# One helper for u in both layers: the high part written by ScalarE from PSUM, the low part as the difference

## The chip, the core and the metric

The kernel runs on one core of a Trainium2 chip. The engines named below are PE (TensorE, the matmuls; PEld is its weight load), DVE (VectorE), ACT (ScalarE), POOL (GpSimd) and SP (SyncE, whose queue issues nearly all DMAs). The metric is the device time of one execution in microseconds (us); less is better.

## The reference, cut to what matters

A trunk of two layers over a sequence of 256 frames of width 2048, inner width 4096. Layer 0 mixes by chunked gated linear attention, layer 1 by a complex diagonal state space (S5). Both begin alike:

```python
shift, scale, gate = jnp.split(mod[i], 3, axis=-1)
u = x * (1.0 + scale[:, None, :]) + shift[:, None, :]
...
h = gla_mixer(u, ...)    # i = 0: proj = u @ w_in
h = s5_mixer(u, ...)     # i = 1: proj = u @ w_in
x = layer_norm(DEEPNORM_ALPHA * x + (1.0 + gate[:, None, :]) * h, ln_g[i], ln_b[i])
```

Only the way in which u is prepared for the first matmuls of each layer differs between the two kernels.

## The kernel before

Every large matmul is made of three products of a reduced type (fp32r): an operand is split in a high part (a cast) and a low part (the operand minus its high part), and high times high, high times low and low times high are summed. So u is kept as four tiles, transposed, with the channels on the partitions: `u0h`, `u0l` in layer 0 and `u1h`, `u1l` in layer 1, 16 slices k of 128 x 256 each.

The weights stream in blocks of 128 x 1024 (two k, called one step kp): SP issues the load (`wload`, L136), ACT casts the high part (L145) and DVE subtracts for the low part (L146); hi and lo sit in rings of buffers. The steps that use u are `mv_step` (L167 to L169, the projection v: 12 matmuls of 128 x 512 a step) and `st_step` (L180 to L182, q and k, z, and in layer 1 su: 24 matmuls of 128 x 256 a step). L167 and L180 take high by high, L168 and L182 the weight's low part, L169 and L181 u's low part.

Layer 0's u comes in blocks of two, two, four and eight k as the conditioning vector's columns arrive. `u_tr` transposes x on PE into a PSUM bank `psx`, two k side by side in one bank (L363). `u_fin` then, for each k: DVE reads PSUM and writes `uf` = x times scale plus shift (L370), ACT casts `uf` to `u0h` (L351), DVE subtracts (L352). Between blocks, the projections v, q and k are computed over the k at hand, and DVE also sums the adaLN rows (L267).

Layer 1's u comes at one place, about 765 to 784 us: after the layer norm's last pass on DVE (L1007) PE transposes into `psn` (L1028, one k per bank, three banks in turn), ACT reads PSUM and writes `vf` (L1030), casts it to `u1h` (L351), and DVE subtracts for `u1l` (L352). Meanwhile PE begins the first group of su, eight steps kp0 to kp7, with the weights of kp0 and kp1 split earlier. Then the temporary pool `tmp0` is closed and `tmp1` takes its place (`tp.close()`, `tp.open("tmp1")`): the tables `rb` of the state space's input matrices (`bload`, L1050 and L1052) lie where `uf` lay, so their loads wait for the last reader of it. From `rb` DVE forms `wb` (`b_pow`, L1090 to L1092), which PE transposes into `pswb` (`b_tr`, L1101).

The order of the instructions on each engine is not that of the source: a scheduler with a cost model of its own sorts them once, and each engine then runs its row in that fixed order, waiting where it must. A change of a few lines can re-sort the row of every engine.

Of the kernel before, what the change touches and what calls it, by code (L numbers as in the profile page):

```python
# [8 lines left out]
F32 = mybir.dt.float32  # L9
F32R = mybir.dt.float32r  # L10
AF = mybir.ActivationFunctionType
ALU = mybir.AluOpType
# [3 lines left out]
P = 128  # L16
D = 2048
E = 4096
T = 256
# [14 lines left out]
def trunk(ctx, tc, x, c, ln_g, ln_b, ada_w, ada_b, gla_w_in, gla_gate_w2, gla_gate_b, gla_norm_g,  # L34
# [3 lines left out]
    V, S, PE = nc.vector, nc.scalar, nc.tensor  # L38
# [32 lines left out]
    tp = Phase()  # L71
    tp.open("tmp0")

    def s8t(name, shape, dt=F32):
        return s8.tile([P] + shape, dt, tag="s8", name=name)
# [4 lines left out]
    def psx(name):  # L80
        return ax.tile([P, 512], F32, tag="ax", name=name)
# [141 lines left out]
    ps = psx("psc")  # L223
# [6 lines left out]
    mods = cp.tile([P, 2, 2, 16], F32, name="mods")  # L230
# [117 lines left out]
    u0 = Parts([s8t(f"u0h{i}", [8, T], F32R) for i in range(2)], [s8t(f"u0l{i}", [8, T], F32R) for i in range(2)])  # L348

    def hilo(hi, lo, src):  # L350
        S.copy(hi, src)  # L351
        V.tensor_tensor(lo, src, hi.bitcast(F32), op=ALU.subtract)  # L352

    vbig = bigp.tile([P, 8448], F32, tag="big", name="vbig")
    vtok = vbig[:, :8192].rearrange("p (j e) -> p j e", j=2)
    win = gla_w_in[0]
# [9 lines left out]
    def u_fin(k2, ps):  # L366
        for kk in range(2):
            k = k2 + kk
            uf = tp.tile([P, T], F32, tag="uf", name=f"uf{k}", bufs=2)
            V.tensor_scalar(uf, ps[:, kk * T:(kk + 1) * T], mods[:, 0, 1, k:k + 1], mods[:, 0, 0, k:k + 1], op0=ALU.mult, op1=ALU.add)  # L370
            hilo(u0.hi(k), u0.lo(k), uf)

    qk = [s8t(f"qk{i}", [8, T]) for i in range(2)]

# [72 lines left out]
    ps = psx("psv2")  # L447
# [8 lines left out]
    got = []  # L456
    ada_now(0, 1, *blocks[0], rows=[8, 4, 4], between=lambda: got.append(u_tr(0)))()
    u_fin(0, got[0])


# [315 lines left out]
    def put_u(k2, at):  # L776
        got = []
        put(at, lambda: got.append(u_tr(k2)))
        put(at, lambda: u_fin(k2, got[0]))
# [50 lines left out]
    for c0, w_, o in ((0, 4, 0), (1, 3, 4), (2, 2, 7)):  # L830
        a = s8t(f"qs{c0}", [8, w_, 64])
# [10 lines left out]
    for h in range(4):  # L842
        ps = psx(f"psst{h}")
# [173 lines left out]
    ab1 = cp.tile([P, 2, 16], F32, name="ab1")  # L1017
# [6 lines left out]
    u1 = Parts([s8t(f"u1h{i}", [8, T], F32R) for i in range(2)], [s8t(f"u1l{i}", [8, T], F32R) for i in range(2)])  # L1024
    for k in range(16):
        ps = psx(f"psn{k}")
        for tt in range(2):
            PE.transpose(ps[:, tt * P:(tt + 1) * P], res0[tt][:, k * P:(k + 1) * P], ident)  # L1028
        uf = tp.tile([P, T], F32, tag="uf", name=f"vf{k}", bufs=2)
        S.activation(uf, ps[:, :T], AF.Identity, scale=ab1[:, 0, k:k + 1], bias=ab1[:, 1, k:k + 1])  # L1030
        hilo(u1.hi(k), u1.lo(k), uf)

    tp.close()
    rp.close()
# [391 lines left out]
    ps = psx("psnb")  # L1426
# [33 lines left out]
```

## Time and profile before

| | |
|---|---|
| time, median of 3 (lowest, highest) | 1846.15 us (1845.58, 1850.67) |
| profiled execution: its own time, span of the trace | 1846.54 us, 1844.7 us |
| busy share of the span, PE / DVE / ACT | 97% / 77% / 49% |
| chain that ended last, share of the span, PE / DVE / DMA / ACT | 86% / 8% / 3% / 2% |

The profiled execution is 0.39 us above the median and within the spread of the three. The span is the traced part of the execution, 1.8 us shorter than its time. PE is busy nearly throughout, so what counts is where it is not: the places in which PE waits for another engine, and the stretches with a lower granted clock.

### The profile page before, as it was taken

Reading aid. Unit: us, or ns where it says so; the run is one execution under the profiler, and the core shown is the slowest. Engines: PE = TensorE matmul, PEld = TensorE weight load, DVE = VectorE, ACT = ScalarE, POOL = GpSimd, SP = SyncE. Lnnn points to the kernel's source line nnn. Section 1 sums busy time; section 2 is a strip of 40 time slices with the busy share of each in tenths; the row PEclk is TensorE's granted clock in tenths of the full one; section 3 lists DMA queues with packets and bytes.
Section 4 is the critical chain, followed back from the end, with each engine's and each line's share of the span. In section 5 each row is a group of like instructions: output and inputs, shape, how many; then the busy total and the mean of one; then the engine's idle time right before and its main releaser. Section 6 shows DMA issues by size and latency. Waiting matters only on the chain.

```text
span 1844.7 us, 33886 instructions
## 1 busy us (share of the span) xinstructions
PE 1795.5 (97%) x13619; PEld 1588.5 (86%) x13619; DVE 1422.5 (77%) x1890; ACT 897.4 (49%) x1252; POOL 72.7 (4%) x78
## 2 busy tenths in 40 slices
PE   7999999999999999999999999999999999999997
PEld 5776897899999888899999999988888888888885
DVE  4877657879989888697899689888677775557556
ACT  5433557556556333654454454545544444444332
POOL 0000000000000000002223200000000000000000
PEclk9999999999999999999999999999999999999999
DMA  9996875889889998465654477899688886668653
GB/s 343 386 333 248 294 244 164 279 261 325 291 286 317 333 353 281 163 220 158 183 151 147 139 214 222 235 246 238 224 276 264 276 271 206 191 189 325 194 184 92
DMA packets 243798, 449.48 MB, mean 244 GB/s; under 512 B 19572, under 2 KB 48942, under 8 KB 242358
## 3 DMA queue, kind: packets, MB, share of 16 engines
q1 hardware_dynamic: 239320, 436.02, 73.9%
q0 software_dynamic: 3552, 10.24, 1.8%
q8 instruction: 107, 1.75, 0.4%
q10 hardware_dynamic: 768, 1.05, 0.2%
q14 instruction: 51, 0.42, 0.1%
HBM read 432.81 MB, written 14.42 MB: 242 GB/s over the span
## 4 chain that ended last, share of the span: by engine, by line
PE 86%; DVE 8%; DMA 3%; ACT 2%; issue 2%; SPq 0%; DVEq 0%; ACTq 0%
PE gl L192 13%; PE gl L193 7%; PE op L168 6%; PE op L167 6%; PE op L169 6%; PE z L182 3%; PE z L180 3%; PE z L181 3%; PE sz L180 3%; PE v L168 3%; PE v L169 3%; PE sz L181 3%; PE sz L182 3%; PE v L167 3%; PE su L180 2%; PE su L182 2%
## 5 line engine op out<-in xcount | busy, mean ns | idle before, releaser
L146 DVE TENSOR_TENSOR logl<-wgl,higl 128x1024 fp32r<-128x1024 f32 x128 | 156.5, 1224 | 115.3 <-ACT higl L145 113.7
L145 ACT CAST higl<-wgl 128x1024 fp32r<-128x1024 f32 x128 | 134.4, 1051 | 172.2 <-PE gl L192 167.9
L192 PE MATMUL gl<-yb,higl 128*128 128x512 f32 x512 | 179.6, 395 | 0.0
L192 PE MATMUL gl<-yp,higl 128*128 128x512 f32 x512 | 179.3, 395 | 0.1
L145 ACT CAST hio<-wo 128x1024 fp32r<-128x1024 f32 x95 | 100.2, 1055 | 155.3 <-PE op L169 127.3
L146 DVE TENSOR_TENSOR loo<-wo,hio 128x1024 fp32r<-128x1024 f32 x95 | 116.2, 1225 | 67.2 <-ACT hio L145 63.7
L315 DVE SCALAR_TENSOR_TENSOR acc<-wa,cs,acc 128x512 f32<-128x512 f32 x217 | 162.2, 748 | 4.8 <-DMA wa<-in_ada_w 2.1
L180 PE MATMUL su<-u1h,hisu 128*128 128x256 f32 x512 | 153.5, 301 | 1.9 <-DVE vv L1108 1.9
L180 PE MATMUL sz<-u1h,hisz 128*128 128x256 f32 x512 | 149.7, 292 | 1.2 <-ACT zs L1290 1.2
L180 PE MATMUL z<-u0h,hiz 128*128 128x256 f32 x512 | 148.7, 290 | 0.0
L182 PE MATMUL su<-u1h,losu 128*128 128x256 f32 x512 | 145.7, 286 | 0.4 <-DVE losu L146 0.4
L181 PE MATMUL su<-u1l,hisu 128*128 128x256 f32 x512 | 145.8, 285 | 0.0
L182 PE MATMUL z<-u0h,loz 128*128 128x256 f32 x512 | 144.9, 283 | 0.6 <-DVE loz L146 0.6
L182 PE MATMUL sz<-u1h,losz 128*128 128x256 f32 x512 | 144.9, 283 | 0.0
L181 PE MATMUL sz<-u1l,hisz 128*128 128x256 f32 x512 | 144.7, 283 | 0.0
L181 PE MATMUL z<-u0l,hiz 128*128 128x256 f32 x512 | 144.7, 283 | 0.0
L193 PE MATMUL gl<-yb,logl 128*128 128x256 f32 x512 | 143.4, 280 | 0.0
L193 PE MATMUL gl<-yp,logl 128*128 128x256 f32 x512 | 142.0, 280 | 0.0
L145 ACT CAST hisz<-wsz 128x1024 fp32r<-128x1024 f32 x64 | 66.9, 1051 | 107.2 <-PE sz L181 55.1
L192 PEld LDWEIGHTS gl<-yb,higl 128*128 128x128 f32 x512 | 96.0, 188 | 22.6
L192 PEld LDWEIGHTS gl<-yp,higl 128*128 128x128 f32 x512 | 95.8, 188 | 22.6 <-issue 0.6
L145 ACT CAST hisu<-wsu 128x1024 fp32r<-128x1024 f32 x64 | 66.7, 1050 | 95.1 <-PE su L181 70.6
(322 smaller groups left out, 5019.8 us busy)
## 6 DMA issues: line engine op xcount, KB each, us to landing
wgl<-in_s_w_glu SPq DMA_DIRECT2D x128, 512.0 KB, 4.7
wa<-in_ada_w SPq DMA_DIRECT2D x116, 512.0 KB, 5.1
wv<-in_gla_w_in SPq DMA_DIRECT2D x64, 512.0 KB, 6.1
wz<-in_gla_w_in SPq DMA_DIRECT2D x64, 512.0 KB, 5.2
wsu<-in_s_w_in SPq DMA_DIRECT2D x64, 512.0 KB, 3.7
wsz<-in_s_w_in SPq DMA_DIRECT2D x64, 512.0 KB, 4.3
wo<-in_s_w_out SPq DMA_DIRECT2D x64, 512.0 KB, 4.5
a<-in_ada_w SPq DMA_DIRECT2D x31, 1024.0 KB, 10.7
```

The costliest lines, as they stand in the source:

```text
L145: S.copy(hi, w)
L146: last_lo[0] = V.tensor_tensor(lo, w, hi.bitcast(F32), op=ALU.subtract).ins
L167: PE.matmul(banks[tt], lhsT=uh, rhs=hi[:, kk, :], start=(k == first), stop=False)
L168: PE.matmul(banks[tt], lhsT=uh, rhs=lo[:, kk, :], start=False, stop=False)
L169: last_mm[0] = PE.matmul(banks[tt], lhsT=ul, rhs=hi[:, kk, :], start=False, stop=(k == last)).ins
L180: PE.matmul(o, lhsT=wh, rhs=u.hi(k), start=(k == first), stop=False)
L181: PE.matmul(o, lhsT=wh, rhs=u.lo(k), start=False, stop=False)
L182: last_mm[0] = PE.matmul(o, lhsT=wl, rhs=u.hi(k), start=False, stop=(k == last)).ins
L192: PE.matmul(banks[f], lhsT=hi[:, kk, fs], rhs=u.both(k), start=(k == 0), stop=False)
L193: PE.matmul(banks[f][:, :T], lhsT=lo[:, kk, fs], rhs=u.hi(k), start=False, stop=(k == last))
L315: V.scalar_tensor_tensor(acc[0], w[:, kk, :], cs[:, k:k + 1], acc[0], op0=ALU.mult, op1=ALU.add)
```

## The change

A new helper `affine_hilo` is used in both layers. ACT computes the affine function straight from PSUM into the high part (L357, an ACTIVATE with scale and bias and a reduced output), DVE computes the same function from the same PSUM slice into `uf` (L358, scale and add in one TENSOR_SCALAR), and DVE subtracts (L359). In layer 0 this replaces DVE's multiply-add, ACT's cast of it, and DVE's subtraction: the same three kinds of work, with the cast's source changed. In layer 1 it replaces ACT's activation, ACT's cast and DVE's subtraction: ACT issues one instruction fewer per k, DVE one more. The two reads of a PSUM slice are put one behind the other, ACT's first (the DVE instruction waits for ACT's). Lines behind L371 are 3 to 5 higher in the kernel after (L1007 becomes L1012, L1050 becomes L1053, L1101 becomes L1104).

```diff
--- before.py
+++ after.py
@@ -351,6 +351,13 @@
         S.copy(hi, src)
         V.tensor_tensor(lo, src, hi.bitcast(F32), op=ALU.subtract)
 
+    def affine_hilo(u, k, src, a, b):
+
+        uf = tp.tile([P, T], F32, tag="uf", name=f"uf{k}", bufs=2)
+        S.activation(u.hi(k), src, AF.Identity, scale=a, bias=b)
+        V.tensor_scalar(uf, src, a, b, op0=ALU.mult, op1=ALU.add)
+        V.tensor_tensor(u.lo(k), uf, u.hi(k).bitcast(F32), op=ALU.subtract)
+
     vbig = bigp.tile([P, 8448], F32, tag="big", name="vbig")
     vtok = vbig[:, :8192].rearrange("p (j e) -> p j e", j=2)
     win = gla_w_in[0]
@@ -366,9 +373,7 @@
     def u_fin(k2, ps):
         for kk in range(2):
             k = k2 + kk
-            uf = tp.tile([P, T], F32, tag="uf", name=f"uf{k}", bufs=2)
-            V.tensor_scalar(uf, ps[:, kk * T:(kk + 1) * T], mods[:, 0, 1, k:k + 1], mods[:, 0, 0, k:k + 1], op0=ALU.mult, op1=ALU.add)
-            hilo(u0.hi(k), u0.lo(k), uf)
+            affine_hilo(u0, k, ps[:, kk * T:(kk + 1) * T], mods[:, 0, 1, k:k + 1], mods[:, 0, 0, k:k + 1])
 
     qk = [s8t(f"qk{i}", [8, T]) for i in range(2)]
 
@@ -1026,9 +1031,7 @@
         ps = psx(f"psn{k}")
         for tt in range(2):
             PE.transpose(ps[:, tt * P:(tt + 1) * P], res0[tt][:, k * P:(k + 1) * P], ident)
-        uf = tp.tile([P, T], F32, tag="uf", name=f"vf{k}", bufs=2)
-        S.activation(uf, ps[:, :T], AF.Identity, scale=ab1[:, 0, k:k + 1], bias=ab1[:, 1, k:k + 1])
-        hilo(u1.hi(k), u1.lo(k), uf)
+        affine_hilo(u1, k, ps[:, :T], ab1[:, 0, k:k + 1], ab1[:, 1, k:k + 1])
 
     tp.close()
     rp.close()
```

The scheduler sorts the rows anew. Three places bear on the prediction.

DVE in layer 1, before: `big` is the normed row that L1007 writes in four pieces, `losu_7583` the low part of the su weights of kp2.

```order
L959 SCALAR_TENSOR_TENSOR rs_5973<-mv_5972,rs_5973 128x1
L1007 TENSOR_SCALAR big_5969<-big_5969,rs_5973 128x512 x4
L146 TENSOR_TENSOR losu_7583<-wsu_7580,hisu_7582 128x1024
L352 TENSOR_TENSOR u1l_7386<-vf_7391,u1h_7384 128x256
L352 TENSOR_TENSOR u1l_7386<-vf_7398,u1h_7384 128x256
```

The same place after, the end of the run of u: L1045 clears the state `sx`, `losu_7613`, `losu_7666` and `losu_7696` are the low parts of kp3, kp4 and kp5, L1093 to L1095 form `wb` from `rb`.

```order
L358 TENSOR_SCALAR uf_7489<-psn_7486,ab_7374 128x256
L358 TENSOR_SCALAR uf_7496<-psn_7493,ab_7374 128x256
L359 TENSOR_TENSOR u1l_7387<-uf_7489,u1h_7385 128x256
L359 TENSOR_TENSOR u1l_7387<-uf_7496,u1h_7385 128x256
L1045 MEMSET sx 128x128 x2
L146 TENSOR_TENSOR losu_7583<-wsu_7580,hisu_7582 128x1024
L146 TENSOR_TENSOR losu_7613<-wsu_7610,hisu_7612 128x1024
L1093 TENSOR_TENSOR wb_7644<-rb_7512 128x128x7
L1094 TENSOR_TENSOR pt_7646<-rb_7512 128x896
L146 TENSOR_TENSOR losu_7666<-wsu_7663,hisu_7665 128x1024
L1095 TENSOR_TENSOR wb_7644<-wb_7644,pt_7646 128x128x7
L146 TENSOR_TENSOR losu_7696<-wsu_7693,hisu_7695 128x1024
```

The low part of kp2's weights stood ahead of all of u; now all 16 pairs of `uf` and `u1l` (32 instructions, of which the last four are shown), and the two clears, stand between L1012 and it.

PE in layer 1, before, around the first transposes of `wb`: `hisu_7725` belongs to kp6, `hisu_7755` to kp7, `su_7516` to `su_7519` are the four PSUM banks of the group.

```order
L180 MATMUL su_7519<-u1h_7385,hisu_7725 128x256
L181 MATMUL su_7519<-u1l_7387,hisu_7725 128x256
L182 MATMUL su_7519<-u1h_7385,losu_7726 128x256
L1101 MATMUL pswb_7651<-ident,wb_7644 128x128 x4
L1101 MATMUL pswb_7657<-ident,wb_7644 128x128 x4
L180 MATMUL su_7516<-u1h_7385,hisu_7755 128x256
```

The same transposes after; `hisu_7612` belongs to kp3 and `hisu_7665` to kp4.

```order
L180 MATMUL su_7519<-u1h_7384,hisu_7612 128x256
L181 MATMUL su_7519<-u1l_7386,hisu_7612 128x256
L182 MATMUL su_7519<-u1h_7384,losu_7613 128x256
L1104 MATMUL pswb_7651<-ident,wb_7644 128x128 x4
L1104 MATMUL pswb_7657<-ident,wb_7644 128x128 x4
L180 MATMUL su_7516<-u1h_7385,hisu_7665 128x256
```

They moved from in front of kp7 to in front of kp4. On SP's queue the `rb` loads moved likewise, from behind four weight loads (kp6, kp7 and two of the next groups) to right behind the store of the normed rows (`dxn`), ahead of the loads of kp6 and kp7.

PE in layer 0, at the fourth to seventh k (about 106 to 111 us), before: `v_1037` and `v_1038` are the two banks of one step with the weights `hiv_1039`, `v_1095` and `v_1096` those of the next with `hiv_1097`.

```order
L363 MATMUL psx_1022<-ident,xrow_152 128x128
L167 MATMUL v_1037<-hiv_1039,u0h_109 128x512
L167 MATMUL v_1038<-hiv_1039,u0h_109 128x512
L167 MATMUL v_1095<-hiv_1097,u0h_109 128x512
L167 MATMUL v_1096<-hiv_1097,u0h_109 128x512
L168 MATMUL v_1037<-lov_1040,u0h_109 128x512
L169 MATMUL v_1037<-hiv_1039,u0l_111 128x512
L167 MATMUL v_1037<-hiv_1039,u0h_109 128x512
```

The same place after.

```order
L370 MATMUL psx_1022<-ident,xrow_152 128x128
L167 MATMUL v_1037<-hiv_1039,u0h_109 128x512
L168 MATMUL v_1037<-lov_1040,u0h_109 128x512
L169 MATMUL v_1037<-hiv_1039,u0l_111 128x512
L167 MATMUL v_1037<-hiv_1039,u0h_109 128x512
L168 MATMUL v_1037<-lov_1040,u0h_109 128x512
L169 MATMUL v_1037<-hiv_1039,u0l_111 128x512
L167 MATMUL v_1038<-hiv_1039,u0h_109 128x512
L168 MATMUL v_1038<-lov_1040,u0h_109 128x512
```

The two matmuls that need the second weight block's high part stood third and fourth; they now stand behind all twelve of the first block. On ACT the order of these casts is the same in both; only `u0h` now needs `psx` alone where it needed DVE's `uf`. In the first block (about 18 us) the first `u0h` now stands ahead of the cast of the first v weights, and the second behind it.

## Rows read from the trace of the kernel before

**Rows 1.** Page, part 1: busy us, share of the span, instructions.

```profile
PE 1795.5 (97%) x13619; PEld 1588.5 (86%) x13619; DVE 1422.5 (77%) x1890; ACT 897.4 (49%) x1252; POOL 72.7 (4%) x78
```

**Rows 2.** Waits of PE, whole span: us in total, times, longest.

```profile
PE pswb L1101 <- DVE wb L1092: 1.9, 2, 1.4
PE su L180 <- DVE vv L1108: 1.9, 1, 1.9
```

**Rows 3.** Timeline, PE, layer 1: start, us, instruction, [idle before <-releaser].

```profile
783.21 0.28 PE L180 MATMUL su<-u1h,hisu 128*128 128x256 f32 x1
...
788.97 0.28 PE L180 MATMUL su<-u1h,hisu 128*128 128x256 f32 x1
...
796.24 1.04 PE L1101 MATMUL pswb<-ident,wb 128*128 128x128 f32 x8
797.03 0.36 PE L180 MATMUL su<-u1h,hisu 128*128 128x256 f32 x1
...
798.77 0.39 PE L182 MATMUL su<-u1h,losu 128*128 128x256 f32 x1 [0.44 <-DVE losu L146]
```

**Rows 4.** Timeline, DVE, layer 1.

```profile
767.08 1.22 DVE L146 TENSOR_TENSOR losu<-wsu,hisu 128x1024 fp32r<-128x1024 f32 x1
...
780.72 0.31 DVE L1042 MEMSET sx<- 128x128 f32 x2 [0.97 <-PE psn L1028]
...
783.32 0.76 DVE L352 TENSOR_TENSOR u1l<-vf,u1h 128x256 fp32r<-128x256 f32 x2
...
788.10 2.09 DVE L1090 TENSOR_TENSOR wb<-rb 128x896 f32<-128x896 f32 x2 [0.96 <-DMA rb<-rec]
```

**Rows 5.** Timeline, SP's queue, layer 1.

```profile
784.16 0.37 SPq L1050 DMA_DIRECT2D rb<-rec  x1
```

**Rows 6.** Tiles uf and vf: ns minimum/median/maximum, first and last start.

```profile
L370 DVE TENSOR_SCALAR uf<-psx,mods x16: 534/539/546, 18.5 to 206.3; 128x256 f32<-128x256 f32 x16
...
L352 DVE TENSOR_TENSOR u0l<-uf,u0h x16: 414/419/426, 20.5 to 208.1; 128x256 fp32r<-128x256 f32 x16
...
L1030 ACT ACTIVATE vf<-psn,ab x16: 553/562/568, 766.2 to 782.4; 128x256 f32<-128x256 f32 x16
L351 ACT CAST u1h<-vf x16: 398/408/417, 767.1 to 783.2; 128x256 fp32r<-128x256 f32 x16
```

**Rows 7.** Timeline, DVE, layer 0, fourth to seventh k.

```profile
106.17 1.00 DVE L370 TENSOR_SCALAR uf<-psx,mods 128x256 f32<-128x256 f32 x2
```

**Rows 8.** Timeline, ACT, layer 0.

```profile
17.65 1.04 ACT L145 CAST hiv<-wv 128x1024 fp32r<-128x1024 f32 x1
...
58.61 0.40 ACT L351 CAST u0h<-uf 128x256 fp32r<-128x256 f32 x1 [2.55 <-DVE uf L370]
...
107.06 1.04 ACT L145 CAST hiv<-wv 128x1024 fp32r<-128x1024 f32 x1
```

**Rows 9.** Timeline, PE, layer 0.

```profile
20.64 1.22 PE L168 MATMUL v<-lov,u0h 128*128 128x512 f32 x2 [0.40 <-DVE lov L146]
...
60.59 0.39 PE L180 MATMUL q<-u0h,hiq 128*128 128x256 f32 x1 [2.35 <-ACT qk L417]
...
105.89 0.71 PE L167 MATMUL v<-hiv,u0h 128*128 128x512 f32 x2
108.16 0.73 PE L167 MATMUL v<-hiv,u0h 128*128 128x512 f32 x2 [1.55 <-ACT hiv L145]
...
111.31 1.92 PE L275 MATMUL psa<-a,cz 128*32 128x512 f32 x16
```

**Rows 10.** Timeline, DVE, layer 0, around 150 us.

```profile
150.03 0.69 DVE L401 TENSOR_TENSOR vbig<-vbig,v 128x512 f32<-128x512 f32 x1 [2.58 <-PE v L169]
```

**Rows 11.** Windows: busy us (count) of PE, PEld, DVE, ACT, POOL, then PEclk.

```profile
767.60:771.00 3.40, 3.40 (x17) 3.22 (x16) 2.13 (x5) 2.26 (x6) 0.00 (x0) 0.50 0.87 319
771.00:774.40 3.40, 3.40 (x31) 3.40 (x31) 1.35 (x4) 3.15 (x9) 0.00 (x0) 1.00 0.41 144
...
840.00:880.00 40.00, 39.96 (x421) 37.74 (x420) 30.10 (x32) 20.41 (x38) 6.74 (x8) 1.00 0.51 154
```

## The prediction

> **What bounds the kernel now.** I read the page's first part, then PE's table of waits, then the timelines of the two places where u is made. The first part shows PE busy 97% of the span and DVE 77% [rows 1], so nothing is won by relieving ACT or DVE as such. Only what PE waits for counts, and each wait is a local matter: a matmul whose operand comes late. The change touches layer 0's u (18 to 208 us) and layer 1's u (766 to 784 us) [rows 6]; what lies elsewhere is re-sorted at most in detail and is carried at zero with an uncertainty of 1 us.
>
> In layer 1 DVE is not ahead of PE by much. Before, it made kp2's low part at 767.08, between the layer norm and u, then one subtraction per k, the last pair at 783.32 [rows 4]. SP issued `rb` at 784.16, as soon as `u1l` left the space free [rows 5]; the data was there at 788.10, when DVE began `wb` [rows 4], so 3.9 us later. PE meanwhile ran its eight steps: from 783.21 to 788.97 there are two of them [rows 3], 2.88 us each, and the first group of su ended where the next begins, at 797.03 [rows 3]. That instant is my yardstick for layer 1.
>
> **Layer 1, part by part.** ACT loses the 408 ns cast for each k and keeps the activation at 562 ns, which now writes the reduced type. DVE keeps the subtraction and gains a TENSOR_SCALAR from PSUM, for which layer 0's L370 at 539 ns is the nearest row [rows 6]. Two of these in a row take 1.00 us by their start and end [rows 7], so one starts 0.46 after the other, 0.91 for two as DVE's own step. Two subtractions take 0.76 from start to end [rows 4], 0.68 as a step. Two k thus cost DVE 1.59 us and sixteen 12.7, from 767.08 (where kp2's low part stood before) to 779.8. To this come waits of DVE for ACT. The order has weight casts of kp3 and kp4, each some 1.04 [rows 8], between ACT's u1h, and PSUM has three banks for `psn`, so u1h of three of the blocks comes late; by stepping both rows against each other I get 1.9 in sum. u ends at 781.7.
>
> Behind the last u1l stand the two clears (0.31, of which 0.2 are in the way [rows 4]) and then kp2's low part at 1.22 [rows 4]: ready at 783.1. PE arrives there when the last `psn` is transposed, which needs a bank that DVE has read (uf of k = 12), about 778.9. This is a new wait of 4.2 us on `losu`, in place of none. Queued behind it on PE are 16 matmuls of kp2 and all of kp3, 4.8 us at 0.12 a matmul, so PE wants `pswb` at 787.9.
>
> `rb` is issued when u1l has ended, 781.7, lands 3.9 later at 785.6, and DVE then does `wb` and `pt` (2.09 for two [rows 4]), kp4's low part (1.22) and L1095 (1.05 like its kind): 789.9 with the queue's small gaps, since kp3's low part is done at 784.4. PE waits there again, 2.0 us. Should the granted clock be at half after the first wait, its cost falls into this second one: a stretch at 0.50 held 17 matmuls, which at the 31 of the stretch behind it take 1.9 of its 3.4 us, a loss of 1.5 [rows 11], less than 2.0. From 789.9 PE has 0.8 of transposes (1.04 for eight, 0.79 to the next start [rows 3]), four steps at 2.88, and 0.8 again: the second group begins at 803.1, 6.1 later than 797.03. The wait of 0.44 in that group [rows 3] then has time to vanish: +5.6 stays. SP's `rb` now also stands ahead of the loads of kp6 and kp7, which are issued some 2 us after 781.7 and are needed only at 795 to 799; that costs nothing unless a load takes over 10 us.
>
> Bounds: with no wait of DVE for ACT, u ends at 779.8 and all behind it comes 1.9 earlier, +3.7. With every DVE instruction at its full length (0.54 and 0.42 [rows 6], sixteen times 0.96 is 15.4) it comes 2.7 later, +8.3. I take +5.6, since the 1.00 for two in a row is a row of the same operation.
>
> What the TENSOR_SCALAR and the ACTIVATE do to each other is seen in no row, because before only one engine reads each slice. The order makes DVE's wait for ACT's, so here the reads follow one another. The Trainium skill, "PSUM — Partial Sum Buffer", section "PSUM bank collisions raise a hardware error ⚠️", says that two engines must not use one bank at once, two reads included; with it the wait stays whatever the engines could do, and no run here tests it.
>
> The activation has its price from layer 1's own row (562 ns, from PSUM, with fp32 output), the cast from SBUF being 408 [rows 6]. The Trainium skill, "Perfetto Trace Analysis", section "Optimizing Scalar/DVE Operations", gives ScalarE a smaller overhead on PSUM (some 51 ns) than on SBUF (some 93). The rows do not show it, the slower of the two reads PSUM, though their operations differ. By the page an ACTIVATE would lie at or below the cast's price, about 0.15 less for each k, and the feed waits would shrink toward the lower bound above; I go by 562.
>
> **Layer 0, part by part.** DVE's and ACT's counts stay; what changes is who waits.
> - First block: ACT did the weight cast at 17.65, before the conditioning vector was there, and now does it behind the first `u0h`, about 18.9 to 19.95. The low part follows 1.22 later, at 21.2 where PE began L168 at 20.64 [rows 8, 9]: +0.6; I count +0.7, with the second `u0h` behind it.
> - Third and fourth k: `u0h` waited 2.55 for DVE until 58.61 [rows 8], and PE 2.35 for the first qk copy behind it [rows 9]. Now the first `u0h` runs at 57.4, but the second shares its bank with DVE's first `uf` and comes behind a weight cast; two activations at 0.56 replace two casts at 0.41. The copy starts 0.35 to 0.45 later: +0.45.
> - Fourth to seventh: between 105.89 and 111.31 PE ran 14 matmuls of 512 columns in 5.42 us, with a wait of 1.55 for a weight cast that stood behind a late `u0h` [rows 9]. At about 0.23 each they take 3.2. The new order needs that cast only later: -2.1.
> - Around 150 us: DVE's addition to `vbig` (0.69 [rows 10]) moves ahead of a weight's low part for which PE waits: +0.75.
> - Last eight k: another wait hides it in both orders, 0.
>
> The sum is -0.2, with bounds of -2.5 (the third part alone, plus half of the wait at 60.59 saved) and +2 (the third part regained by nothing).
>
> **Sum.** 5.6 - 0.2 is +5.4; stretches of half clock may fall a little differently, so I take +5.3 and 1.5 [rows 11] either way. On the profiled execution's 1846.54 that is 1851.8; its 0.39 above the median of 1846.15 is noise of the runs, so against the median it is 1851.4. A difference within 0.3%, here 5.5 us, can't be told from none; the forecast lies at that very edge.
>
> **The rivals.**
> A. The loss is larger, slower than before beyond the edge. One mechanism: DVE's instructions run at their full lengths because each `uf` waits afresh for ACT's read, so no overlap is left. It decides from 0.3 us more a pair. For it: all 16 `uf` now have a wait on ACT, and before, each pair of u1l came at ACT's pace. Against: DVE's pair at 1.00 in layer 0. +8.3 - 0.2 gives +8.1, 1854.3.
> B. The reads don't cost waits: ACT is so far ahead that u1h is always there (its load falls by 16 x 0.41 = 6.5 us). +3.7 - 0.2 gives 1849.6. Against: the weight casts in between, and three banks.
> C. The loss is given back, not slower at all: where PE comes late, later waits shrink. Those behind layer 1's u are 1.4 (the longest on `wb`) and 1.9 on `vv` [rows 2], and if the latter goes, so might a half-clock stretch of 1.5 [rows 11]: 4.8 of 5.3, 1846.6. Against: DVE is busy 30.1 of 40 us from 840 to 880 [rows 11], so its lag does not last, and its later work hangs on PE's own progress, which shifts with it.
> D. The change doesn't do what the order says, for instance a re-sorted later stage costs or saves as much as all this: either sign, beyond +-4; I give it a small chance.
>
> **How the numbers follow.** Forecast 0.55, A 0.15, B 0.14, C 0.11, D 0.05. The forecast's own range is 1849 to 1854; it straddles the edge at 1851.7, slightly more of it below: 0.29 same, 0.26 slower. B and C are same (0.25 together, but 0.04 of C and B faster through a better layer 0 and clock), A is slower, D half faster, half slower (0.03, 0.02). Slower 0.26 + 0.15 + 0.02 = 0.43, faster 0.04 + 0.03 = 0.07, same 0.50. The range from 1846.3 to 1855.0 holds the forecast, A, B and most of C.
>
> **What would show it.** Right: a PE wait on DVE's `losu` at L182 of about 4 us near 779 to 783; DVE's row from 767 to 782 filled with pairs of TENSOR_SCALAR and subtraction; another PE wait of about 2 at `pswb` near 790; the second group of su at about 803; in layer 0 the wait at 108.16 gone and that at 60.59 slightly longer. Wrong: no wait on `losu`, or DVE's pairs at 1.9 us instead of 1.6, a second group of su before 800 or after 806, or a shift at 797 that is no longer there at the end of the trace.

## The result

The changed kernel takes 1850.71 us (median of 22 runs) and the kernel before, timed beside it, 1847.84 (22 runs). The ratio is 1.0021 with a 95% interval of 1.0013 to 1.0028: slower by 3.9 us, between 2.4 and 5.2, and so by less than the 0.3% named in the prediction. The plain difference of the two medians is 2.9 us, inside that interval. Forecast were 5.3 us, just above it. The sign is right, and so are the place and the size of the main wait; part of the loss came back later, which the forecast had put at nothing, so part of the closeness of the total is luck.

### The profile page after: what moved, and what is told of

Same layout as the page of the kernel before. It is cut to its first block, busy times and chain, and to the rows that moved or that the text cites. A ratio compares the mean times of both kernels' runs of the same rounds, so it can differ in the third digit from the quotient of the medians.

```text
span 1847.8 us, 33893 instructions
## 1 busy us (share of the span) xinstructions
PE 1797.6 (97%) x13619; PEld 1590.7 (86%) x13619; DVE 1429.6 (77%) x1906; ACT 896.3 (49%) x1236; POOL 69.4 (4%) x78
## 4 chain that ended last, share of the span: by engine, by line
PE 85%; DVE 8%; DMA 3%; issue 2%; ACT 2%; SPq 0%; DVEq 0%; ACTq 0%
PE gl L192 13%; PE gl L193 7%; PE op L168 6%; PE op L167 6%; PE op L169 6%; PE z L182 3%; PE z L180 3%; PE z L181 3%; PE v L168 3%; PE v L169 3%; PE v L167 3%; PE sz L180 3%; PE sz L181 2%; PE sz L182 2%; PE su L180 2%; PE su L182 2%
```

## The profile after, beside that of before

The first part of the page of the changed kernel, columns as in [rows 1]: DVE has 16 instructions more, ACT 16 fewer, PE's busy time is 2 us up.

```profile
PE 1797.6 (97%) x13619; PEld 1590.7 (86%) x13619; DVE 1429.6 (77%) x1906; ACT 896.3 (49%) x1236; POOL 69.4 (4%) x78
```

PE's waits in the changed kernel, in us in total, times, longest. The first row is new (before, one wait of 0.4 stood there); the last was 3.9 before.

```profile
PE su L182 <- DVE losu L146: 4.1, 1, 4.1
...
PE q L180 <- ACT qk L422: 2.6, 1, 2.6
...
PE v L167 <- ACT hiv L145: 1.8, 1, 1.8
PE psy L1263 <- DMA mt<-dk: 1.4, 2, 1.1
```

DVE's timeline in layer 1, the end of the run of u. Against [rows 4], kp2's low part comes not at 767.08 but behind the last u1l and the clears, in the first of the two `losu` of the row at 783.85.

```profile
782.00 0.99 DVE L358 TENSOR_SCALAR uf<-psn,ab 128x256 f32<-128x256 f32 x2
782.90 0.75 DVE L359 TENSOR_TENSOR u1l<-uf,u1h 128x256 fp32r<-128x256 f32 x2
783.63 0.31 DVE L1045 MEMSET sx<- 128x128 f32 x2
783.85 2.71 DVE L146 TENSOR_TENSOR losu<-wsu,hisu 128x1024 fp32r<-128x1024 f32 x2
786.64 1.09 DVE L1093 TENSOR_TENSOR wb<-rb 128x896 f32<-128x896 f32 x1
```

PE's timeline there. The yardstick of [rows 3], the first matmul of su's second group, moved from 797.03 to 805.75.

```profile
785.07 0.58 PE L182 MATMUL su<-u1h,losu 128*128 128x256 f32 x1 [4.12 <-DVE losu L146]
...
805.75 0.36 PE L180 MATMUL su<-u1h,hisu 128*128 128x256 f32 x1
```

Two windows right behind that wait (columns as in [rows 11]): a granted clock of 0.50 and 0.55, so nearly all of both at the lower of the clock's two levels (1.2 instead of 2.4 GHz), with 19 matmuls in the second where a window at full clock has 32. In this trace the half clock there lasts about 6.8 us; in other traces it lasts about 3.4 at the same place, and I call that one stretch.

```profile
784.60:788.00 3.40, 2.93 (x13) 2.93 (x14) 3.32 (x4) 0.67 (x2) 0.88 (x1) 0.50 0.71 194
788.00:791.40 3.40, 3.40 (x19) 3.40 (x19) 3.40 (x4) 1.05 (x1) 0.00 (x0) 0.55 0.88 271
```

To see where the time goes over the whole span, I matched each PE matmul with its like before, took the difference of their starts, and then its median over stretches of 20 us. I call this the lag, always against the first trace of before. From it, for all traces that follow (us; "layer 1" is the lag at 820 less that at 740):

| trace | at 40 | at 120 | at 200 | at 740 | at 820 | layer 1 | at 1200 | at 1300 | at 1800 |
|---|---|---|---|---|---|---|---|---|---|
| after | 1.7 | 0.1 | 1.6 | 1.5 | 8.1 | 6.6 | 7.9 | 4.5 | 3.0 |
| after, again | 0.5 | 0.3 | 1.9 | 1.8 | 5.8 | 4.0 | 5.3 | 2.4 | 1.0 |
| before, again | 0.1 | 0.2 | 1.7 | 1.7 | 1.1 | -0.5 | 1.2 | -0.1 | -0.9 |
| layer 0 alone | 1.4 | -0.3 | 1.3 | 1.3 | 1.4 | 0.1 | 2.2 | 1.4 | 1.1 |
| layer 1 alone | 0.5 | 0.6 | 0.5 | 0.8 | 6.2 | 5.4 | 5.5 | 1.8 | 1.6 |
| layer 1, low parts first | 0.1 | 0.2 | 0.2 | 0.2 | 1.2 | 1.1 | 2.3 | 2.6 | 1.3 |
| layer 0 from k = 4 | -0.5 | -0.8 | 0.9 | 1.2 | 1.6 | 0.5 | 1.9 | 1.1 | -0.7 |
| layer 1, TENSOR_SCALAR twice | 1.4 | 1.4 | 4.4 | 4.4 | 17.3 | 12.8 | 17.4 | 19.7 | 19.0 |
| layer 1, both reads on ACT | 0.7 | 0.8 | 3.8 | 3.9 | 6.2 | 2.2 | 6.4 | 3.8 | 3.0 |
| whole change, low parts first | 1.6 | 0.0 | 1.5 | 1.4 | 1.5 | 0.1 | 0.7 | 0.7 | -0.3 |
| layer 0, k = 4 to 7 | 0.7 | -1.1 | 0.6 | 0.6 | 0.8 | 0.2 | 0.9 | -2.5 | -3.5 |

The row "before, again" is the measure of chance: an unchanged kernel is off by 1.7 in the middle, and 2.0 of change lie between 820 and 1800. What it is off by in the middle is one stretch of half clock behind a wait for `lov`, the low part of the v weights (the second fence line has columns as in [rows 11]). The first trace of before has the same wait (1.94 at 161.76) without it:

```profile
161.92 0.50 PE L168 MATMUL v<-lov,u0h 128*128 128x512 f32 x1 [1.93 <-DVE lov L146]
...
163.20:166.60 3.40, 3.40 (x9) 2.21 (x7) 3.33 (x5) 0.00 (x0) 0.00 (x0) 0.51 0.01 4
```

With the TENSOR_SCALAR twice and with both reads on ACT, where layer 0 is also as before, two such stretches follow the waits there, which is 3.0 of the 4.4 and 3.8 at 200. So the first trace of before happened to be a quick one in layer 0, and a lag against it holds up to 3 us of that chance. The column "layer 1" leaves out what arose before 740.

## The experiments

The theory: what costs is that kp2's low part stands behind all of layer 1's u, so that PE waits for DVE's whole run; layer 0 adds a little. The rivals: the added work or the two reads of one bank cost wherever it stands; layer 0 costs the most or nothing; what comes back late is chance.

**Layer 0 alone.** The edit leaves the helper in `u_fin` and restores layer 1's loop:

```diff
-        affine_hilo(u1, k, ps[:, :T], ab1[:, 0, k:k + 1], ab1[:, 1, k:k + 1])
+        uf = tp.tile([P, T], F32, tag="uf", name=f"vf{k}", bufs=2)
+        S.activation(uf, ps[:, :T], AF.Identity, scale=ab1[:, 0, k:k + 1], bias=ab1[:, 1, k:k + 1])
+        hilo(u1.hi(k), u1.lo(k), uf)
```

> The change in layer 0 alone, layer 1 as before. In the trace of the changed kernel PE lags the kernel before by 1.55 us between layer 0's u and layer 1's: +1.7 from the first block (0.5 from the later weight cast, 1.1 from a stretch of half clock that runs to 26.4 instead of 23.4 us), +0.3 at 60 us, -2.5 at 108, +1.9 between 112 and 160. Theory (the lag is made by the order in layer 0): the same +1.5 at 700 us here, no new wait on losu in layer 1, and a time 0 to 1.5 us above before. Rival (layer 0 costs nothing and its lag in the one trace was chance): 0 +- 0.3 at 700 us.

Measured: the lag at 740 is 1.3, near the 1.5 of the theory, and layer 1 adds nothing (0.1). The ratio is 0.9997 (0.9985 to 1.0009), so -0.6 us (-2.8 to +1.7): in the time layer 0 can't be told from none. The shape of the lag in layer 0 (a fall of about 2 at 108, a rise of about 1.9 from there to 160) is the same in all four traces with the whole of it changed, so it is the order's doing. Its net of 1.3 is no more than the 1.7 by which the unchanged kernel is off, so the rival that the net is chance is not refuted.

**Layer 1 alone.** The edit is the reverse: layer 1's loop as changed, `u_fin` as before.

> The change in layer 1 alone, layer 0 as before. Theory (the loss is layer 1's): a wait of PE of 4.1 us on losu at kp2, half clock behind it, PE later by 6 to 7 us at 820 us; of these some 3 to 5 come back where PE waits for DMAs at 1240 to 1260 us and in the last projections, so the time is 1.5 to 4 us above before. Rival (the lag isn't returned, what came back in the one trace was chance): 6 to 7 us above before. Rival (layer 0 matters as much): below 1 us.

Measured: ratio 1.0017 (1.0005 to 1.0030), 3.1 us; layer 1 adds 5.4 and 4.6 come back between 820 and 1800. The wait is the same to the hundredth:

```profile
783.55 0.58 PE L182 MATMUL su<-u1h,losu 128*128 128x256 f32 x1 [4.12 <-DVE losu L146]
```

So layer 1 makes the loss: without layer 0's part the time is nearly that of the whole change.

**Layer 1 alone, low parts first.** The same work, with the low parts of kp2 and kp3 at another place in DVE's row. `early_split(kp)` (its definition is left out below) loads and splits the weights of one step: kp0 to kp2 ahead of the loop, kp3 at its middle, and u's DVE instructions are bound to follow. The rows of PE and ACT are re-sorted with it: PE's first transposes of `wb` stand behind 158 matmuls of su, where the changed kernel has 96 and the kernel before 168.

```diff
...
+    with tc.issue_after(normed1):
+        early_split(2)
     for k in range(16):
+        if k == 8:
+            early_split(3)
...
+        with tc.issue_after(last_lo[0]):
+            affine_hilo(u1, k, ps[:, :T], ab1[:, 0, k:k + 1], ab1[:, 1, k:k + 1])
```

> As the run with layer 1 alone, but kp2's low part is put ahead of all of u on VectorE and kp3's between the eighth and ninth k; the added TENSOR_SCALARs and both reads of PSUM stay. Theory (the place of kp2's low part in VectorE's row makes the loss): no wait on losu at kp2, PE 0 to 3 us later than before at 820 us (what is left is wb, which VectorE reaches about 1 to 2.5 us later than PE wants it at 790). Rival (the loss is VectorE's added work or the two engines' reads of one bank): still 5 to 7 us at 820 us, with the wait on another step's low part.

Measured: ratio 1.0001 (0.9989 to 1.0012), layer 1 adds 1.1. No wait on `losu` is left at kp2; PE's only waits from 764 to 800 are these (before, the first two had their like of 3.51 and 0.44; the third is new):

```profile
766.00 0.55 PE L1047 MATMUL psn<-ident,big 128*128 128x128 f32 x3 [3.51 <-DVE big L1014]
...
766.99 0.74 PE L180 MATMUL su<-u1h,hisu 128*128 128x256 f32 x4 [0.44 <-ACT u1h L357]
...
768.96 1.14 PE L1047 MATMUL psn<-ident,big 128*128 128x128 f32 x4 [1.24 <-DVE uf L358]
```

The 16 added instructions and the reads of one bank are all still there, and 4.3 of the 5.4 us are gone, so the rival that they cost as such falls. In the time the two runs' intervals still overlap (layer 1 alone 1.0005 to 1.0030); the same edit on the whole change, below, parts them.

**Layer 0 from k = 4.** `u_fin` uses the helper for k of 4 and above only; all else is before.

```diff
+            if k2 >= 4:
+                affine_hilo(u0, k, ps[:, kk * T:(kk + 1) * T], mods[:, 0, 1, k:k + 1], mods[:, 0, 0, k:k + 1])
+                continue
```

> The new helper only for layer 0's k = 4 to 15, the first four k and all of layer 1 as before. Theory (the helper's gain is the freed ScalarE at 108 us, its loss in layer 0 is the first block and the row behind 112 us): no lag at 60 us, -2 to -2.5 at 112 us, then +0.9 to +1.9 again to 160 us, so -1.5 to 0 at 700 us, and a time 0 to 1.5 us below before. Rival (the gain at 108 us hangs on the first blocks): 0 or above at 112 us.

Measured: ratio 0.9990 (0.9981 to 1.0000), at the limit of what can be told. The lag at 112 is not -2 to -2.5 but about -1.3, and -0.8 at 120: at 84 us, behind a wait of 1.2 that before has too, this trace shows a stretch of half clock that costs 1.6, and the gain comes on top of it (from about 1.2 at 100 to -0.8 at 120). It is then given back by 1.9 to 160 us.

**Layer 1, TENSOR_SCALAR twice.** The suspected cost doubled, with the order of DVE's row otherwise that of layer 1 alone (PE's transposes into `psn` and two of ACT's weight casts are re-sorted):

```diff
         V.tensor_scalar(uf, src, a, b, op0=ALU.mult, op1=ALU.add)
+        V.tensor_scalar(uf, src, a, b, op0=ALU.mult, op1=ALU.add)
```

> As the run with layer 1 alone, but each TENSOR_SCALAR of layer 1's u is issued twice into the same tile, so VectorE has 16 more of them, 0.46 us each as a step, at most 7.4 in sum; the order is otherwise the same. Theory (VectorE's length between the layer norm and kp2's low part sets the loss one for one): the wait on losu grows from 4.1 to 9.5 to 11.5 us and the lag at 820 us from 5.7 to 11 to 13. What comes back behind 1000 us: if it is PE's wait for DMAs that a later PE finds done, again about 4 us and not more, so 7 to 9 above before; if it is a share of the lag, about 8, so 4 to 6 above before; if it was chance, nothing, 11 to 13 above.

Measured: ratio 1.0059 (1.0043 to 1.0075), 10.9 us against 3.1. Layer 1 adds 12.8 against 5.4, so 7.4 for 16 instructions at 0.46. One for one, as expected: DVE reaches kp2's low part 10.7 us later than with layer 1 alone (793.03 against 782.33), of which 3.6 are already there at 740. The wait on `losu` did not grow, though, and this part of my expectation failed: PE now waits 5.1 us in sum ahead of it, for DVE to free the `psn` banks, because the last six blocks of transposes now stand together behind the first 56 matmuls of su.

```profile
786.90 1.11 PE L1036 MATMUL psn<-ident,big 128*128 128x128 f32 x4 [1.72 <-DVE uf L359]
...
794.25 0.58 PE L182 MATMUL su<-u1h,losu 128*128 128x256 f32 x1 [4.21 <-DVE losu L146]
```

The lag did not come back either: from 820 to 1800 it grew by 1.7, with a stretch of half clock at 1240 in it that layer 1 alone does not have. Of the three cases the time, 10.9 us above before (7.9 to 13.9), lies with the third, chance (11 to 13); it rules out that a share of the lag comes back (4 to 6) and only just leaves room for a fixed 4 us (7 to 9).

**Layer 1, both reads on ScalarE.** DVE is spared the added work, ACT writes both tiles from PSUM:

```diff
+        S.activation(u1.hi(k), ps[:, :T], AF.Identity, scale=ab1[:, 0, k:k + 1], bias=ab1[:, 1, k:k + 1])
         S.activation(uf, ps[:, :T], AF.Identity, scale=ab1[:, 0, k:k + 1], bias=ab1[:, 1, k:k + 1])
-        hilo(u1.hi(k), u1.lo(k), uf)
+        V.tensor_tensor(u1.lo(k), uf, u1.hi(k).bitcast(F32), op=ALU.subtract)
```

> Layer 0 as before; in layer 1 ScalarE writes both u1h and uf straight from PSUM with two ACTIVATEs, VectorE only subtracts. VectorE's instructions are as many as before and the cast no longer waits for the activation's end; ScalarE has 0.15 us more for each k. Theory (the loss is VectorE's 16 added instructions and the order that the scheduler makes of them): kp2's low part stays ahead of u, no wait on losu at kp2, lag at 820 us within 2 us of before, time within 0.15% of before. Rival (two reads of a PSUM bank are what costs): a lag of 4 us or more at 820 us.

Measured: ratio 1.0007 (0.9995 to 1.0018). The lag at 820 is 6.2, but 3.9 of it are there at 740, 3.0 from two stretches of half clock in layer 0; layer 1 adds 2.2, just over the 2 expected and well under the 4 of the rival, which falls. With DVE's row spared, kp2's low part stays ahead of u, and what is left is ACT's own length: PE waits 1.30 for a weight cast that stands behind all of u on ACT. The time is not better than before.

**The kernel before, again, and the changed kernel, again.** Two unchanged kernels, one more execution of each.

> The kernel before, unchanged, a second profile. It shows what one trace's waits are worth: if the waits of PE for mt (3.9 us in the first trace, two of them near 1240 and 1260) and the rate of the last projections come out the same within 1 us, what the changed kernel gets back there is its lag's doing; if they differ by 2 us or more, it is chance of the DMAs.

> The changed kernel, unchanged, a second profile. Expected of either theory: the lag at 820 us is 8 us again, as all of it stands in waits between engines. If what comes back behind 1000 us is the lag's doing, it is 4 to 5 us again; if it is chance, it lies anywhere from 0 to 5.

Measured: the wait on `losu` is there once more at 4.12, but the lag at 820 is 5.8, not 8, so that expectation failed. Each of three runs of half clock (at 20, at 768 and behind the `losu` wait) lasts about 3.4 us in this trace, and about 6.8 in the first; on the other hand this trace has one more, of 3.4 us at 85, behind a wait of 1.2. The second window behind the wait on `losu` is at full clock:

```profile
785.00:788.40 3.40, 3.40 (x19) 3.40 (x18) 3.40 (x4) 1.71 (x3) 0.00 (x0) 0.52 0.75 191
788.40:791.80 3.40, 3.40 (x32) 3.40 (x31) 3.40 (x5) 0.40 (x1) 0.00 (x0) 1.00 1.02 365
```

PE's waits for `mt` sum to 2.5 in before again and to 0.8 in after again. Between 3.9 and 2.5 lies chance alone; the difference of 1.4 is between the 1 that would have spoken for the lag and the 2 that would have spoken for chance, so this expectation decides nothing. From 820 to 1800 the changed kernel gets back 4.8 here and 5.0 in the first trace, the kernel before 2.0 against itself.

**The whole change, low parts first.** The edit of the third experiment on the changed kernel.

> The whole change, both layers, with kp2's low part ahead of layer 1's u on VectorE and kp3's between its eighth and ninth k. Theory (the two layers add, and layer 1's loss is the place of the low parts): no wait of 4 us on losu at kp2; of the 4.5 to 6.5 us that layer 1 costs in the changed kernel 1 or less stays, layer 0's 0.5 to 2 us stay, so 0 to 2 us above before and 2 to 4 below the changed kernel. Rival (with both layers changed the loss comes back in another wait): 3 us or more above before.

Measured: ratio 0.9994 (0.9983 to 1.0004), which lies below the changed kernel's 1.0013 to 1.0028 altogether. Layer 1 adds 0.1, and no wait on `losu` is left there. Against before that is -1.1 us (-3.1 to +0.7) where 0 to 2 above were expected, and some 5 below the changed kernel where 2 to 4 were. DVE's row shows the place, ahead of the first `uf`:

```profile
768.52 1.22 DVE L146 TENSOR_TENSOR losu<-wsu,hisu 128x1024 fp32r<-128x1024 f32 x1
769.65 0.99 DVE L358 TENSOR_SCALAR uf<-psn,ab 128x256 f32<-128x256 f32 x2
```

**Layer 0, k = 4 to 7.** As the fourth experiment, with `if k2 in (4, 6):`.

> The new helper for k = 4 to 7 of layer 0 alone, where ScalarE's wait for VectorE cost 1.55 us on PE; all else as before. Theory: the wait at 108 us goes and its issue loss, -2 to -2.5 at 112 us; VectorE's row to 160 us is still re-sorted and gives 0.9 to 1.9 back, so -1.5 to 0 at 145 to 200 us, and a time of 0 to 1.5 us below before, at the limit of what can be told. Rival (the re-sorted row there is due to the last eight k): the gain of 2 us stays to 200 us.

Measured: ratio 0.9988 (0.9977 to 1.0000), the lowest of all, not clear of no change. From 80 to 120 us the lag falls by 1.9; to 160 it rises by 1.8. The last eight k are thus not what re-sorts the row there, and the rival falls. At 200 the lag is 0.6, above the -1.5 to 0 expected; it holds 0.7 that are there at 40, ahead of the changed part.

## Why the prediction held, step by step

- *A new wait of 4.2 on kp2's low part.* Right. Measured 4.12, in all three traces with this order. DVE's pairs ran at 0.99 or 1.00 for two where nothing came between, its waits for ACT summed to 1.6 (1.9 forecast), and u ended at 783.6, which less the lag of 1.5 is 782.1 (781.7 forecast). With that rival A (no overlap left) and rival B (no waits for ACT) both fall. The activation with the reduced output kept its price:

```profile
L357 ACT ACTIVATE u1h<-psn,ab x16: 556/564/567, 767.9 to 781.0; 128x256 fp32r<-128x256 f32 x16
```

That is 564 ns against 562 before. The forecast was right to go by that row, but its remark that the rows show no smaller overhead on PSUM is a misreading: the activation also takes scale and bias from tiles, which the cast from SBUF does not. Rows of the kernel before that compare like with like, 128 x 256 each: an ACTIVATE from PSUM with no such operand, one from SBUF with none, and one from PSUM with a scale from a tile.

```profile
L882 ACT ACTIVATE sqt<-pso x28: 362/374/384, 373.2 to 561.2; 128x256 f32<-128x256 f32 x28
L1351 ACT ACTIVATE sg<-sg x32: 405/416/427, 1341.2 to 1663.4; 128x256 f32<-128x256 f32 x32
L877 ACT ACTIVATE og<-pso,vt x32: 429/467/475, 369.3 to 560.9; 128x256 f32<-128x256 f32 x32
```

So PSUM is some 40 ns cheaper than SBUF (374 against 416), and each operand from a tile adds 93 to 95 (374, 467, 562). The Trainium skill ("Perfetto Trace Analysis", "Optimizing Scalar/DVE Operations") gives ScalarE a smaller overhead per instruction on PSUM (about 51 ns) than on SBUF (about 93). The trace agrees that PSUM is the cheaper, here by 42 ns. What fails is the step from there to an activation no dearer than the cast: the 0.15 less that I had drawn from it does not come.
- *`rb` 3.9 later, PE waits 2.0 again at `pswb`, and half clock falls into that wait.* Partly wrong. `rb` was issued at 783.72 and `wb` began at 786.64, at most 2.9 later, and no wait stands at `pswb` there. Its place was taken by half clock: about 6.8 us of it behind the wait in the first trace, a cost of some 3 us, where the forecast had 1.5 that would vanish in a wait of 2.0. Layer 1 came out at 4.0 with one stretch each at 768 and behind `losu` (after again), at 5.4 with one and two (layer 1 alone) and at 6.6 with two and two (the first trace). The mean is 5.3, against 5.6 forecast; that it comes so near although the second wait is missing is luck.
- *DVE's length sets it one for one.* Shown, by the doubled instruction (7.4 for 16).
- *Layer 0: -0.2.* Its net stays open. The four traces with the whole of layer 0 changed lag by 1.3 to 1.8 at 740, but against one trace of before: the other five traces with layer 0 as before stand at 0.2 to 4.4 there, 2.2 in the mean. The time of layer 0 alone, -0.6 us (-2.8 to +1.7), holds both -0.2 and +1.7. The terms can be read singly. The first block, +0.7: PE's wait there is 1.8 where it was 1.3, so +0.5; the lag at 40 is 0.5 to 1.7, but -0.5 to 1.4 also where that block is as before. The third and fourth k, +0.45: 0.2 more wait (2.57 against 2.35). The fourth to seventh, -2.1: -1.8 to -2.0. Around 150 us, +0.75: +1.8 to +2.0 between 120 and 160, in all six traces with this part changed. This last term is mis-sized: I priced one instruction of the re-sorted row and not the row, which from 124 us on loses in steps of 0.2 to 0.3 as well. What may offset it is that none of these six traces has the half clock at 157 to 169 that three of the six with the old order have; six are too few to call that an effect.
- *The loss is not given back.* Wrong for part of it. The four traces with a layer-1 lag of 2.2 to 6.6 lose 3.2 to 5.0 of their lag from 820 to 1800, where rival C had named 4.8 and other places (`wb`, `vv`). Most of it falls at 1240 to 1300, where PE waits less for `mt`. The half clock behind the wait on `vv`, one of rival C's places, is indeed missing in both traces of the changed kernel (the first trace of before has it from 1003.0 to 1006.6): 1.5 are gained there, and 0.8 lost again at once in a new wait at `pswb`. But six traces with lags of 0.8 to 1.6 at 820 change by +0.1 to -4.2 there too, -1.8 in the mean, and the one with a lag of 17 by +1.7. Behind about 820 us the order of before and after is the same on every engine, so it is no re-sorting. What a lag of 5 to 8 gains over chance there stays open; I can't say that such a lag causes it.

So the term that makes the loss, layer 1's, was right in its cause and near in its size. The return, put at nothing, came out at 3 to 5 against the first trace of before, of which some 1.8 is what six other traces change by in the mean as well; and layer 0's net is not measured well enough to call its -0.2 right or wrong. One of the forecast's signs of being wrong, a shift at 797 that is no longer there at the end of the trace, is met in good part: 8.1 became 3.0, and 5.8 became 1.0. The total was nearer than its parts.

## What to carry to other kernels

Where a scheduler sets the order, a change of a few lines is judged by what it moves on the engine that feeds the bottleneck: here 16 instructions cost 0.1 to 1.1 us when the weights' low parts stood ahead of and between them, and 4.0 to 6.6 when these stood behind them. To avoid such a loss, bind the order at the one place where the bottleneck waits, and count a re-sorted row as a whole. Several profiles of the unchanged kernel show which part of a difference is chance before a story is built on it: here the single trace that all others were held against was itself a lucky one in one place and a slow one in another.

## What was not expected of the hardware

The granted clock of one and the same kernel differs between executions: behind the same wait (3.51 us at `psn`, 4.12 at `losu`) PE runs at half clock for about 3.4 us or for about 6.8. In two of the twelve traces, of different kernels, half clock also followed a wait of 1.2 at 84 us that is in the others without it, and in three of the six with layer 0 as before it followed waits of 1.8 to 1.9 at 157 to 165. A stretch can cost 1.6 us (the one at 85 in after again) or next to nothing (0.1 for the second one at 768 in layer 0 alone, much of which fell into PE's wait for `psn`), and a few of them are as large as the whole effect measured here.
